# One weight sum of every seven-product group, made in DRAM by a copy and an adding transfer

## The chip, the cores and the metric

One core of one Trainium2 chip runs the whole kernel. The metric is the device time in microseconds of one execution; three executions of the kernel before took 1473.48, 1473.88 and 1474.7 us, the median is 1473.88 us. The profile is of one execution. Its engines are called PE (matrix products), PEld (the load of the stationary operand of a product), DVE, ACT and POOL (elementwise work), and SP (which here issues DMA transfers). SPq, ACTq and POOLq are the instruction queues of those engines.

## The reference

One decoder layer on 256 tokens of width 2048, everything in float32:

```
u = RMSNorm(h);  P = u @ W_in               # 2048 x 12320, split into z | x,B,C | dt | q | k | v
y_ssm = norm(SSD_scan(silu(conv(x,B,C)), softplus(dt)) * silu(z))
y_att = mixture of dilated causal windows over q, k, v     # 16 heads of 128
h = h + RMSNorm(concat(y_ssm, y_att) @ W_out)              # W_out 4096 x 2048
h = h + RMSNorm(relu(RMSNorm(h) @ W_up)^2 @ W_down)        # W_up 2048 x 8192, W_down 8192 x 2048
```

Nearly all of the time goes to the five products with `W_in`, `W_out`, `W_up` and `W_down`, whose weights are all read once.

## The kernel before, in words

**A float32 product in three.** Each weight tile `raw` of 2 x 128 x 512 floats (512 KB, the function `fetch`, one DMA on SP's queue, L149) is split into `hi` (ACT rounds it, L139) and `lo = raw - hi` (DVE, L140). The activations are held split as well. A product is then three matmuls: high by high, high by low, low by high (L262 to L264 in `row_tile`; L393 and L396 in `products`, where the weights are the stationary operand). Four `raw` buffers and five pairs of `hi` and `lo` let DMA, ACT and DVE run ahead of PE by a few tiles.

**Seven products for eight.** A group of the 2 x 2 blocks of 128 tokens and 128 weight rows, by two column blocks of 512, would take eight products. `seven` (L311) takes seven, by the Winograd form of Strassen's scheme: it needs four sums of weights. With `A = raw_a`, `B = raw_b` (the two column blocks `ca` and `cb` of the same two row blocks 0 and 1) DVE makes, in L320 to L325 through `add_in_line` (L225), `e0 = A0 + B0`, `e1 = e0 + B1`, `t4 = e1 + A1`, and in place `B0 = B0 + B1`. Then the tiles A, e, (B0+B1, B1) and t4 are split as above. The combined results are put together by `combine_new` or `combine_onto`. 59 groups are done so: 8 for the values, 9 in `W_out`, 21 in `W_up`, 21 in `W_down`. The others go by `row_tiles`. `unit` runs through one pair of column blocks in a written order of groups.

**The order of the work.** A scheduler sorts the instructions of each engine: higher priority first (`tc.high_priority`), and what depends on data waits by semaphore. `tc.issue_after(i)` adds an order edge behind the instruction `i`, without a semaphore. Each engine then runs its list strictly in order. The first 350 us do the projections for B, C, x, z of the SSD heads, with convolution and scan worked in between; then queries, keys, values and attention; then `W_out`, `W_up` and `W_down`. The first use of `seven` is with the values, some 400 us in.

**Where the step sits that the prediction speaks of.** The first RMSNorm's scale `rstd` is made early: DVE sums (L543) and `rm` (L133), then POOL raises it to the power of -1/2 (L134, in `rsqrt_mean`). `over_partitions` (L546) spreads it: DVE makes `dg` from `rstd` (L551), PE multiplies `ones` by `dg` (L552), DVE copies the result to `rbc` (L553). The convolution (`conv`, L652) uses `rbc` for every block; it has POOL set three columns of `pad` to zero (L655) and DVE do the rest. POOL has 67 instructions in all. It issues no DMA in the kernel before.

Of the kernel before, what the change touches and what calls it, by code (L numbers as in the profile page):

```python
# [10 lines left out]
F32 = mybir.dt.float32  # L11
# [3 lines left out]
ALU = mybir.AluOpType  # L15

P = 128
# [20 lines left out]
COL_V = COL_K + NH * DH  # L38
NB = 512
KB = 2  # L40
MASKED = -1.0e30
PAIRS = ((128, 1), (512, 4), (2048, 16))
AHEAD = 1_000_000
# [7 lines left out]
FIRST = 3  # L51
UP_SEVENS = (2, 4, 5)
V_SEVENS = (1, 3, 5, 6)


def constants():
# [18 lines left out]
def hymba_layer(ctx: ExitStack, tc: tile.TileContext, x, norm_mix_pre, w_in, conv_w, conv_b, dt_bias, a_log,  # L75
                d_skip, ssm_norm_w, w_out, norm_mix_post, norm_mlp_pre, w_up, w_down, norm_mlp_post,
                consts, out):
    nc = tc.nc
    w_in, w_out, w_up, w_down = w_in[0], w_out[0], w_up[0], w_down[0]
# [61 lines left out]
        return (nc.scalar.activation(hi, src, AF.Copy, scale=scale),  # L141
                nc.vector.scalar_tensor_tensor(lo, src, scale, hi.bitcast(F32), op0=ALU.mult, op1=ALU.subtract))

    def fetch(src, k0, c0, step=KB, into=None):

        raw = wp.tile([P, KB, NB], F32, name="raw", bufs=RAWS) if into is None else into
        for j in range(0, KB, step):
            rs = slice((k0 + j) * P, (k0 + j + step) * P)
            nc.sync.dma_start(raw[:, j:j + step], src[rs, c0:c0 + NB].rearrange("(k p) n -> p k n", p=P))  # L149
        return raw  # L150
# [13 lines left out]
    room = {}  # L164
# [22 lines left out]
        room["acts"] = acts  # L187
        sums_of.clear()

    def fetch_next(src, k0, c0):  # L190

        if room["raw"] is None:
            return fetch(src, k0, c0)
        turn = room["turn"]
        room["turn"] += 1
        n = KB * (turn % (RAWS + (NK - SUMS) // KB - 1) - RAWS)
        return fetch(src, k0, c0, into=None if turn < 0 or n < 0 else room["raw"][:, n:n + KB])

    def parts():
        return [wp.tile([P, KB, NB], F32R, name=n, bufs=BUFS) for n in ("hi", "lo")]  # L200
# [2 lines left out]
    product = {}  # L203
# [5 lines left out]
    line = {}  # L209
# [10 lines left out]
        with in_line():  # L220
            line["act"], line["dve"] = split(hi, lo, raw)

    def add_in_line(dst, a, b):
        with in_line():
            line["dve"] = nc.vector.tensor_tensor(dst, a, b, op=ALU.add)  # L225

    def weights(src, k0, c0, fetch=fetch):

# [82 lines left out]
    def seven(src, ca, cb, k, acc, more, first, last):  # L311


        ch, cl = sums_of_acts(k)
        h_, l_, r = room["acts"](k * KB)
        with tc.high_priority(offset=AHEAD):
            raw_a = fetch_next(src, k * KB, ca)
            raw_b = fetch_next(src, k * KB, cb)
            e, t4 = sum_tile(), tmp()
            add_in_line(e[:, 0], raw_a[:, 0], raw_b[:, 0])  # L320
            add_in_line(e[:, 1], e[:, 0], raw_b[:, 1])
            hl_a = parts()
# [12 lines left out]

        def summed(i):
            return ch[:, i], cl[:, i]

        for dst, (a_h, a_l), (hi, lo), j, own in (
                (more[0], block(0, 0), hl_a, 0, True), (acc[0], block(1, 0), hl_a, 1, False),  # L340
                (more[1], summed(1), hl_e, 0, True), (more[2], summed(2), hl_e, 1, True),
                (more[3], summed(0), hl_b, 0, True), (acc[1], summed(3), hl_b, 1, False),
                (acc[2], block(1, 1), hl_t, 0, False)):
            nc.tensor.matmul(dst, a_h, hi[:, j], start=own and first, stop=False)  # L344
            nc.tensor.matmul(dst, a_h, lo[:, j], start=False, stop=False)  # L345
            nc.tensor.matmul(dst, a_l, hi[:, j], start=False, stop=own and last)  # L346
# [12 lines left out]
    def order_of(ks, by_seven):  # L359
        return [(k, k in by_seven) for k in ks]  # L360
# [445 lines left out]
    def keys_too(hb):  # L806
        return queries(COL_Q + hb * NB, rbq), queries(COL_K + hb * NB, rbc)
# [11 lines left out]
    def two_values(vb):  # L819

        if vb:
            room["own"] = deque(mp.tile([P, NT, NB], F32, name="tk", bufs=3)[:, t] for t in range(NT))
        room["sum"] = mp.tile([P, 4, S], F32, name="cT", bufs=5).rearrange("p (k f) s -> p k (f s)", k=KB)
        values = [mp.tile([P, NT, NB], F32, name="tk", bufs=3) for _ in range(2)]
        more = [psmall(), bank(), psmall(), bank()]
        acc = [bank() for _ in range(2 * NT)]

        def end(b):
            def at_end(t, a):
                with tc.high_priority(offset=AHEAD):  # L830
# [5 lines left out]
        unit(w_in[:, COL_V:], vb, order_of(range(7), V_SEVENS), (7,), acc, more,  # L836
             lambda x: combine_new([[v[:, t] for t in range(NT)] for v in values], x), 0, (end(0), end(1)))
        return values

# [236 lines left out]

    in_place_of_u()
    acc = [bank() for _ in range(2 * NT)]
    early = 5
    for k in range(early):  # L1080
# [31 lines left out]
    def whole(n):  # L1112
        def at_end(t, a):
# [1 line left out]
                mixed(n, t, a)  # L1115
        return at_end

    unit(w_out, 0, order_of(range(early, 14), (6, 9, 12)), (14, 15), acc, more,
         lambda x: combine_new(in_mw(0), x), 0, (whole(0), whole(1)), first=False)
    for n in (2, 3):  # L1120
        load_wpost(norm_mix_post, n)
    acc, more = more, acc
# [9 lines left out]
    def first_hidden(t, acc):  # L1132
# [11 lines left out]
    unit(w_out, 2, order_of((0, 6, 1, 9, 2, 12, 3, 4, 5, 8, 7, 10), (6, 9, 12, 4, 8, 10)), (11, 13, 14, 15), acc, more,  # L1144
         lambda x: combine_new(in_mw(2), x), ending=mix_to_up)
    begun = ended.pop()
    over_partitions(rbc, rmlp)
# [88 lines left out]
    for hf in range(2):  # L1236
        if hf:
            in_place_of_h(act_u)
        for fb in range(0 if hf else 2, 8, 2):
            unit(w_up[:, hf * 4096:], fb, order_of(range(6), UP_SEVENS), (6, 7), acc, more,  # L1240
                 lambda x: combine_new(room["shared"], x), 0, (up_end(fb, 0), up_end(fb + 1, 1)))
            acc, more = more, acc
        if hf == 0:
            in_place_of_h(part)
            unit(w_down, 0, order_of(range(14), (4, 6, 9, 11, 13)), (14, 15), acc, more,
                 lambda x: combine_new(in_mw(0), x), 0, (onto(0), onto(1)))
            unit(w_down, 2, order_of((0, 1, 4, 2, 6, 3, 9, 5, 11, 7, 13, 8), (4, 6, 9, 11, 13)), (10, 12, 14, 15), more, acc,
                 lambda x: combine_new(in_mw(2), x), 0, (onto(2), onto(3)))
    new_h()

# [11 lines left out]
    in_place_of_u()  # L1262
    for n in range(2):
        load_wpost(norm_mlp_post, n)
    unit(w_down[4096:], 0, order_of(range(14), (3, 6, 8, 11, 13)), (14, 15), acc, more,
         lambda x: combine_onto(0, x), 0, (complete(0), complete(1)))
    for n in (2, 3):
        load_wpost(norm_mlp_post, n)
    waiting.append(copies(of_h, in_dram, 1))
    unit(w_down[4096:], 2, order_of((0, 1, 3, 2, 6, 4, 8, 5, 11, 7, 13, 9), (3, 6, 8, 11, 13, 9)), (10, 12, 14, 15), more, acc,  # L1270
         lambda x: combine_onto(2, x), LAG_DOWN, (complete(2), finish))


# [21 lines left out]
```

## Time and profile before

| | |
|---|---|
| median of three runs | 1473.88 us |
| span of the profiled execution, first to last instruction | 1471.1 us |
| own time of the profiled execution | not listed apart; the three timed runs stand 2.4 to 3.6 us above the span |
| PE busy | 1461.2 us |
| DVE busy | 1239.6 us |
| ACT busy | 861.1 us |
| POOL busy | 47.8 us |
| bytes moved by DMA | 287.31 MB |

A row of a group reads: line, engine, operation, output and input tiles, shapes, number of instructions, then busy time and the mean of one in ns, then the idle time of the engine just before them and who ended it. A row of a timeline reads: start, length, engine, line, operation, and in brackets the idle time ahead of it and its releaser. A row of the stretches reads: from and to, length, then busy time and number of instructions of PE, PEld, DVE, ACT and POOL, the granted clock, the DMA engines' busy share, and GB/s. Busy time of PE runs up to modelled ends of its pipelined matmuls.

### The profile page before, as it was taken

Reading aid. Unit: us, or ns where it says so; the run is one execution under the profiler, and the core shown is the slowest. Engines: PE = TensorE matmul, PEld = TensorE weight load, DVE = VectorE, ACT = ScalarE, POOL = GpSimd, SP = SyncE. Lnnn points to the kernel's source line nnn. Section 1 sums busy time; section 2 is a strip of 40 time slices with the busy share of each in tenths; the row PEclk is TensorE's granted clock in tenths of the full one; section 3 lists DMA queues with packets and bytes.
Section 4 is the critical chain, followed back from the end, with each engine's and each line's share of the span. In section 5 each row is a group of like instructions: output and inputs, shape, how many; then the busy total and the mean of one; then the engine's idle time right before and its main releaser. Section 6 shows DMA issues by size and latency. Waiting matters only on the chain.

```text
span 1471.1 us, 20006 instructions
## 1 busy us (share of the span) xinstructions
PE 1461.2 (99%) x7216; PEld 1231.4 (84%) x7216; DVE 1239.6 (84%) x1849; ACT 861.1 (59%) x1188; POOL 47.8 (3%) x67
## 2 busy tenths in 40 slices
PE   9999999999999999999999999999999999999998
PEld 8888888888888888888888888888888888888886
DVE  6798797898497696588989989889887898989998
ACT  7475675465456565555557566655554666665553
POOL 0003100210000000000000000000000000000000
PEclk9999999999999999999999999999999999999999
DMA  7665566555657476566657566655665666576853
GB/s 272 208 205 182 179 184 194 174 172 167 177 168 207 122 208 192 191 229 210 204 177 237 165 194 201 210 175 191 213 223 174 201 201 205 172 235 202 273 200 114
DMA packets 151299, 287.31 MB, mean 195 GB/s; under 512 B 11696, under 2 KB 14624, under 8 KB 151200
## 3 DMA queue, kind: packets, MB, share of 16 engines
q1 hardware_dynamic: 143472, 272.50, 58.9%
q10 hardware_dynamic: 7728, 13.54, 2.8%
q8 instruction: 56, 0.92, 0.3%
q14 instruction: 43, 0.35, 0.1%
HBM read 281.78 MB, written 4.23 MB: 194 GB/s over the span
## 4 chain that ended last, share of the span: by engine, by line
PE 94%; DVE 3%; issue 1%; ACT 1%; DMA 1%; POOL 0%; POOLq 0%; SPq 0%; ACTq 0%; DVEq 0%
PE acc L393 17%; PE acc L262 12%; PE acc L263 12%; PE acc L264 12%; PE acc L396 9%; PE acc L345 4%; PE acc L346 4%; PE acc L344 4%; PE ps L263 3%; PE ps L262 3%; PE ps L264 3%; PE ps L346 2%; PE ps L344 2%; PE ps L345 2%; DVE lo L140 1%
## 5 line engine op out<-in xcount | busy, mean ns | idle before, releaser
L139 ACT ACTIVATE hi<-raw 128x1024 fp32r<-128x1024 f32 (+1 forms) x477 | 499.0, 1053 | 387.9 <-PE acc L393 111.9
L140 DVE TENSOR_TENSOR lo<-raw,hi 128x1024 fp32r<-128x1024 f32 (+1 forms) x477 | 579.9, 1220 | 135.7 <-ACT hi L139 127.9
L393 PE MATMUL acc<-ua,hi 128*128 128x512 f32 x680 | 186.3, 402 | 0.0
L393 PEld LDWEIGHTS acc<-ua,hi 128*128 128x128 f32 x680 | 119.7, 189 | 18.7
L262 PE MATMUL acc<-hi,ua 128*128 128x512 f32 x280 | 112.0, 400 | 0.0
L396 PEld LDWEIGHTS acc<-ua,lo 128*128 128x128 f32 x680 | 99.8, 189 | 11.6
L264 PE MATMUL acc<-hi,ua 128*128 128x512 f32 x280 | 109.3, 391 | 0.0
L263 PE MATMUL acc<-lo,ua 128*128 128x512 f32 x280 | 109.3, 390 | 0.0
L396 PE MATMUL acc<-ua,lo 128*128 128x256 f32 x680 | 102.9, 281 | 0.0
L262 PE MATMUL acc<-hi,sh 128*128 128x512 f32 x224 | 88.7, 397 | 0.0
L264 PE MATMUL acc<-hi,sl 128*128 128x512 f32 x224 | 87.3, 390 | 0.0
L263 PE MATMUL acc<-lo,sh 128*128 128x512 f32 x224 | 87.3, 390 | 0.0
L139 ACT ACTIVATE hi<-e 128x1024 fp32r<-128x1024 f32 x51 | 54.1, 1062 | 55.5 <-DVE e L225 50.3
L393 PE MATMUL acc<-uc,hi 128*128 128x512 f32 x272 | 77.6, 398 | 0.0
L263 PE MATMUL acc<-lo,ah 128*128 128x512 f32 x168 | 65.5, 390 | 0.4 <-DVE lo L140 0.4
L264 PE MATMUL acc<-hi,al 128*128 128x512 f32 x168 | 65.4, 389 | 0.0
L262 PE MATMUL acc<-hi,ah 128*128 128x512 f32 x168 | 65.4, 389 | 0.0
L264 PEld LDWEIGHTS acc<-hi,ua 128*128 128x128 f32 x280 | 52.6, 188 | 11.6
L140 DVE TENSOR_TENSOR lo<-e,hi 128x1024 fp32r<-128x1024 f32 x51 | 62.0, 1216 | 0.0
L262 PEld LDWEIGHTS acc<-hi,ua 128*128 128x128 f32 x280 | 52.6, 188 | 10.4 <-ACT ua L141 0.3
L263 PEld LDWEIGHTS acc<-lo,ua 128*128 128x128 f32 x280 | 52.7, 188 | 10.0
L264 PE MATMUL acc<-hi,uc 128*128 128x512 f32 x144 | 56.0, 389 | 0.0
(475 smaller groups left out, 3060.9 us busy)
## 6 DMA issues: line engine op xcount, KB each, us to landing
raw<-in_w_in_dram SPq DMA_DIRECT2D x189, 512.0 KB, 3.6
raw<-in_w_up_dram SPq DMA_DIRECT2D x128, 512.0 KB, 3.9
raw<-in_w_down_dram SPq DMA_DIRECT2D x110, 512.0 KB, 4.7
raw<-in_w_out_dram SPq DMA_DIRECT2D x46, 512.0 KB, 4.2
uc<-in_w_out_dram SPq DMA_DIRECT2D x18, 512.0 KB, 4.5
uc<-in_w_down_dram SPq DMA_DIRECT2D x18, 512.0 KB, 5.1
bc<-acs_d ACTq DMA_DIRECT2D x8, 512.0 KB, 4.5
xs<-in_x_dram SPq DMA_DIRECT2D x8, 256.0 KB, 6.3
```

Source lines behind the costliest of these rows:

```text
L139: return (nc.scalar.activation(hi, src, AF.Copy), nc.vector.tensor_tensor(lo, src, hi.bitcast(F32), op=ALU.subtract))
L140: nc.vector.tensor_tensor(lo, src, hi.bitcast(F32), op=ALU.subtract))
L262: nc.tensor.matmul(dst, a_h[:, r, ts], hi[:, j], start=begin and j == 0, stop=False)
L263: nc.tensor.matmul(dst, a_h[:, r, ts], lo[:, j], start=False, stop=False)
L264: product[t] = nc.tensor.matmul(dst, a_l[:, r, ts], hi[:, j], start=False, stop=end and j == KB - 1)
L344: nc.tensor.matmul(dst, a_h, hi[:, j], start=own and first, stop=False)
L345: nc.tensor.matmul(dst, a_h, lo[:, j], start=False, stop=False)
L346: nc.tensor.matmul(dst, a_l, hi[:, j], start=False, stop=own and last)
L393: nc.tensor.matmul(acc[f], hi[:, j, f * P:(f + 1) * P], u(k0 + j), start=k0 + j == 0, stop=False, skip_group_check=True)
L396: nc.tensor.matmul(acc[f][:, 0], lo[:, j, f * P:(f + 1) * P], u(k0 + j)[:, 0], start=False, stop=k0 + j == NK - 1, skip_group_check=True)
```

## The change

The sum `B0 + B1` of every `seven` is not made by DVE. For each group `next_pair` asks POOL's queue for two transfers: a copy of the 128 x 512 block `B0` from the weights to a tile `d` in DRAM (256 KB), and a second transfer that adds the block `B1` to it. `seven` loads `d` in place of `B0` (a DMA of its own on SP's queue, and one more for `B1`, 256 KB each), and DVE then makes `e1 = A0 + d` and `e0 = e1 - B1`. That is three sums by DVE instead of four, 59 times. `plan` writes down the order in which groups come; four pairs are asked for at first, between the first and the second block of queries and keys, and then one more each time that `seven` fetches one. The copy stands inside `issue_after` edges to the last matmuls of `row_tile`. All calls of `next_pair` but the first four are made inside the `tc.high_priority` block of `seven`, since `pair_of` is an argument there.

```diff
-    def fetch(src, k0, c0, step=KB, into=None):
+    def fetch(src, k0, c0, step=KB, into=None, pair=None):
         raw = wp.tile([P, KB, NB], F32, name="raw", bufs=RAWS) if into is None else into
+        if pair is not None:
+            nc.sync.dma_start(raw[:, 0], pair)
+            nc.sync.dma_start(raw[:, 1], src[(k0 + 1) * P:(k0 + 2) * P, c0:c0 + NB])
+            return raw
...
+    def plan(name, src, n, order, by_seven):
+        orders[name, n] = order_of(order, by_seven)
+        pairs.extend((src, n * NB, k) for k in order if k in by_seven)
+
+    def next_pair():
+        if not pairs:
+            return
+        src, ca, k = pairs.pop(0)
+        cb = slice(ca + NB, ca + 2 * NB)
+        d = dram.tile([P, NB], F32, name=f"pair{len(paired)}")
+        with ExitStack() as order:
+            for t in product:
+                order.enter_context(tc.issue_after(product[t].ins))
+            nc.gpsimd.dma_start(d, src[k * KB * P:(k * KB + 1) * P, cb])
+        nc.gpsimd.dma_start(d, src[(k * KB + 1) * P:(k * KB + 2) * P, cb], accum_op=ALU.add)
+        paired.append((src, ca, k, d))
+
+    def pair_of(src, ca, k):
+        next_pair()
+        s_, c_, k_, d = paired[turn_of["pair"]]
...
+        return d
...
         with tc.high_priority(offset=AHEAD):
             raw_a = fetch_next(src, k * KB, ca)
-            raw_b = fetch_next(src, k * KB, cb)
+            raw_b = fetch_next(src, k * KB, cb, pair_of(src, ca, k))
             e, t4 = sum_tile(), tmp()
-            add_in_line(e[:, 0], raw_a[:, 0], raw_b[:, 0])
-            add_in_line(e[:, 1], e[:, 0], raw_b[:, 1])
+            add_in_line(e[:, 1], raw_a[:, 0], raw_b[:, 0])
+            add_in_line(e[:, 0], e[:, 1], raw_b[:, 1], ALU.subtract)
             hl_a = parts()
             split_in_line(*hl_a, raw_a)
             add_in_line(t4, e[:, 1], raw_a[:, 1])
-            add_in_line(raw_b[:, 0], raw_b[:, 0], raw_b[:, 1])
...
+    for _ in range(PAIRS_AHEAD):
+        next_pair()
     qk.append(keys_too(1))
```

The rest of the diff hands the orders through `plan` to `unit` and changes no group.

More of the change, by code (lines that the diff above doesn't have):

```diff
@@ L40 @@
 KB = 2
+EARLY = 5
 MASKED = -1.0e30
@@ L53 @@
 V_SEVENS = (1, 3, 5, 6)
+PAIRS_AHEAD = 4
 def constants():
@@ L196, in fetch_next @@
         n = KB * (turn % (RAWS + (NK - SUMS) // KB - 1) - RAWS)
-        return fetch(src, k0, c0, into=None if turn < 0 or n < 0 else room["raw"][:, n:n + KB])
+        return fetch(src, k0, c0, into=None if turn < 0 or n < 0 else room["raw"][:, n:n + KB], pair=pair)
     def parts():
@@ L221, in split_in_line, with add_in_line, order_of @@
             line["act"], line["dve"] = split(hi, lo, raw)
-    def add_in_line(dst, a, b):
+    def add_in_line(dst, a, b, op=ALU.add):
         with in_line():
-            line["dve"] = nc.vector.tensor_tensor(dst, a, b, op=ALU.add)
+            line["dve"] = nc.vector.tensor_tensor(dst, a, b, op=op)
+    pairs = []
+    w_v, w_ups, w_downs = w_in[:, COL_V:], [w_up[:, hf * 4096:] for hf in range(2)], [w_down, w_down[4096:]]
+    orders = {}
+    def order_of(ks, by_seven):
+        return [(k, k in by_seven) for k in ks]
+    def plan(name, src, n, order, by_seven):
[13 more added lines that the diff above has]
+        paired.append((src, ca, k, d))
+    paired = []
+    def pair_of(src, ca, k):
+        next_pair()
+        s_, c_, k_, d = paired[turn_of["pair"]]
+        assert (s_ is src) and (c_, k_) == (ca, k), (c_, k_, ca, k)
+        turn_of["pair"] += 1
+        return d
+    turn_of = {"pair": 0}
     def weights(src, k0, c0, fetch=fetch):
@@ L834, in end @@
             return at_end
-        unit(w_in[:, COL_V:], vb, order_of(range(7), V_SEVENS), (7,), acc, more,
+        unit(w_v, vb, orders["v", vb], (7,), acc, more,
              lambda x: combine_new([[v[:, t] for t in range(NT)] for v in values], x), 0, (end(0), end(1)))
@@ L1078, in hymba_layer @@
     acc = [bank() for _ in range(2 * NT)]
-    early = 5
-    for k in range(early):
+    for k in range(EARLY):
         for b in range(2):
@@ L1116, in whole @@
         return at_end
-    unit(w_out, 0, order_of(range(early, 14), (6, 9, 12)), (14, 15), acc, more,
+    unit(w_out, 0, orders["out", 0], (14, 15), acc, more,
          lambda x: combine_new(in_mw(0), x), 0, (whole(0), whole(1)), first=False)
@@ L1142, in first_hidden @@
         split(sh[:, 0:4, ts], sl[:, 0:4, ts], p.rearrange("p (f s) -> p f s", f=4))
-    unit(w_out, 2, order_of((0, 6, 1, 9, 2, 12, 3, 4, 5, 8, 7, 10), (6, 9, 12, 4, 8, 10)), (11, 13, 14, 15), acc, more,
+    unit(w_out, 2, orders["out", 2], (11, 13, 14, 15), acc, more,
          lambda x: combine_new(in_mw(2), x), ending=mix_to_up)
@@ L1239, in hymba_layer @@
         for fb in range(0 if hf else 2, 8, 2):
-            unit(w_up[:, hf * 4096:], fb, order_of(range(6), UP_SEVENS), (6, 7), acc, more,
+            unit(w_ups[hf], fb, orders[("up", hf), fb], (6, 7), acc, more,
                  lambda x: combine_new(room["shared"], x), 0, (up_end(fb, 0), up_end(fb + 1, 1)))
@@ L1264, in hymba_layer @@
         load_wpost(norm_mlp_post, n)
-    unit(w_down[4096:], 0, order_of(range(14), (3, 6, 8, 11, 13)), (14, 15), acc, more,
+    unit(w_downs[1], 0, orders[("down", 1), 0], (14, 15), acc, more,
          lambda x: combine_onto(0, x), 0, (complete(0), complete(1)))
@@ L1269, in hymba_layer @@
     waiting.append(copies(of_h, in_dram, 1))
-    unit(w_down[4096:], 2, order_of((0, 1, 3, 2, 6, 4, 8, 5, 11, 7, 13, 9), (3, 6, 8, 11, 13, 9)), (10, 12, 14, 15), more, acc,
+    unit(w_downs[1], 2, orders[("down", 1), 2], (10, 12, 14, 15), more, acc,
          lambda x: combine_onto(2, x), LAG_DOWN, (complete(2), finish))
```

22 lines of the change are left out of this document (16 added, 6 removed).

## The prediction

> **What bounds the kernel now.** I read the page's head and busy times first, then PE's list of waits, then a piece of PE's timeline inside a seven-product group.
>
> ```profile
> span 1471.1 us, 20006 instructions
> ...
> PE 1461.2 (99%) x7216; PEld 1231.4 (84%) x7216; DVE 1239.6 (84%) x1849; ACT 861.1 (59%) x1188; POOL 47.8 (3%) x67
> ...
> PE 94%; DVE 3%; issue 1%; ACT 1%; DMA 1%; POOL 0%; POOLq 0%; SPq 0%; ACTq 0%; DVEq 0%
> ```
>
> The span is 1471.1 us; the timed runs' median, 1473.88, stands 2.8 us above it. PE is busy for 1461.2 us, and 94% of the chain that ended last is PE. Busy time of PE is modelled, so I look at the starts:
>
> ```profile
> 1010.90 0.39 PE L344 MATMUL acc<-hi,ah 128*128 128x512 f32 x1
> 1011.13 0.39 PE L345 MATMUL acc<-lo,ah 128*128 128x512 f32 x1
> 1011.36 0.39 PE L346 MATMUL acc<-hi,al 128*128 128x512 f32 x1
> ```
>
> A matmul starts every 0.23 us, also inside `seven`, back to back. And PE's waits for other engines are these, longest first:
>
> ```profile
> PE ps L1168 <- ACT dg L1167: 2.3, 1, 2.3
> PE ps L444 <- DVE half L433: 1.1, 1, 1.1
> PE ps L961 <- DVE ha L952: 0.9, 1, 0.9
> PE acc L263 <- DVE lo L140: 0.4, 1, 0.4
> PE acc L345 <- DVE lo L140: 0.3, 1, 0.3
> ```
>
> PE waits 0.7 us in all for a `lo` of DVE, though DVE is 84% busy. So PE's stream of matmuls is the bound, and DVE's share is hidden under it. The change leaves the number of matmuls as it is.
>
> **What it removes.** One addition of this row per group:
>
> ```profile
> L225 DVE TENSOR_TENSOR raw<-raw 128x512 f32<-128x512 f32 x54 | 36.8, 682 | 0.0
> ```
>
> ```profile
> L225 DVE TENSOR_TENSOR uc<-uc x5: 678/682/685, 689.9 to 1427.5; 128x512 f32<-128x512 f32 x5
> ```
>
> 59 groups (54 and, in the tile `uc`, 5) by 0.682 us are 40 us of DVE. Beside a PE that waits 0.7 us for `lo`, they are worth at most that: I take 0, with -0.7 as the end. The remaining three additions keep their length and order. The second DMA of SP costs an issue of 0.37 us (L149's row, below) by 59, 22 us of a queue that mostly waits for buffers: 0. The bytes into SBUF are the same.
>
> **What it adds, and where.** The trace of before has no DMA from POOL and none with an addition. What decides is where these stand. In the built program of after, POOL's list (line numbers of the changed file; 256 is the copy, 257 the adding transfer, 136 is the old L134) begins so after its constants:
>
> ```
> L256 DMACopy pair<-in_w_in    x4
> L257 DMACopy pair<-in_w_in    x4   each waits for its own copy
> L256 DMACopy pair<-in_w_out   x4
> L257 DMACopy pair<-in_w_out   x4   each waits for its own copy and for the adding transfer four before
> ...                                (13 such rounds of 4 + 4)
> L256 DMACopy pair<-in_w_down  x3
> L136 TensorTensor rstd<-rm,half
> ```
>
> The order edges of `issue_after` go to matmuls, and PE's list isn't POOL's: no copy carries a wait for PE. With `seven`'s priority and nothing to wait for, 55 of the 59 pairs have moved to the front of POOL's list: 55 copies and 52 adding transfers, "some groups ahead" by up to 1400 us. Only the first four pairs keep their place. Behind all this stands `rstd`, the scale of the first norm. In before:
>
> ```profile
> 38.45 0.70 POOL L134 TENSOR_TENSOR rstd<-rm,half 128x2 f32<-128x2 f32 x1 [2.45 <-DVE rm L133]
> ...
> 46.94 0.28 DVE L551 TENSOR_SCALAR dg<-cst,rstd 128x128 f32<-128x128 f32 x1
> ```
>
> `rstd` was there at 39 us and DVE used it at 47 us. In the built list of after, DVE's `dg` stands behind the 36th `lo` instead of the 19th, and PE's L552 stands after the 20th matmul of L264, at the place that before's PE reached here:
>
> ```profile
> 97.10 0.39 PE L262 MATMUL acc<-hi,ub 128*128 128x512 f32 x1
> 97.32 0.39 PE L263 MATMUL acc<-lo,ub 128*128 128x512 f32 x1
> 97.55 0.39 PE L264 MATMUL acc<-hi,ub 128*128 128x512 f32 x1
> ```
>
> So PE can do 97 us of before's work without `rstd`. If POOL comes to it at a time T later than that, DVE stands at `dg`, every later `lo` is queued behind it on DVE, and PE stops when its tiles are used up. The delay is T - 97, plus the catching up after it. Slower weights before T don't add to it; they only eat into the same wait.
>
> **T, from both sides.** Nearest rows: SP's issue; the queue that carries the weights, and transfers of 256 KB (the first `xs`, then into DRAM, out of DRAM, to the output) with us to landing last; and the first stretches, with the DMA engines' share and GB/s last:
>
> ```profile
> L149 SPq DMA_DIRECT2D raw<-in_w_in_dram x195: 367/368/690, 1.7 to 569.6; - x195
> ```
>
> ```profile
> q1 hardware_dynamic: 143472, 272.50, 58.9%
> ...
> xs<-in_x_dram SPq DMA_DIRECT2D x8, 256.0 KB, 6.3
> ...
> h_d<-ha ACTq DMA_DIRECT2D x6, 256.0 KB, 4.3
> ha<-h_d ACTq DMA_DIRECT2D x6, 256.0 KB, 6.9
> ...
> out_dram<-ha SPq DMA_DIRECT2D x2, 256.0 KB, 2.3
> ```
>
> ```profile
> 0.00:95.00 95.00, 93.79 (x540) 82.31 (x541) 72.00 (x140) 59.30 (x99) 1.53 (x11) 1.00 0.70 225
> ...
> 10.00:20.00 10.00, 10.00 (x63) 8.88 (x62) 7.13 (x12) 7.40 (x16) 0.00 (x0) 1.00 1.05 385
> ```
>
> - Low end: issues cost what SP's cost, transfers land as the fastest row. A round is 8 x 0.37 + 2.3 = 5.3 us; 13 rounds are 69 us, less than 97.
> - By the DMA engines' time: 0.589 x 16 x 1471.1 / 143472 is 96.6 ns for a packet of 2 KB, so 128 rows on 16 engines are 0.77 us. 55 copies are 42 us. An adding transfer has two rows to read for each that it writes; between 0.77 and 1.55 us each, 52 are 40 to 81 us. The weights up to 97 us want 0.70 x 97 = 68 us (the same stretch). With the 16 engines always full, T is 42 + 40 + 68 = 150 us to 42 + 81 + 68 = 191 us.
> - High end: a round takes a copy's landing of 6.9 us and an adding landing of twice that in turn, 20.7 us; 13 rounds are 269 us.
>
> I take T = 170, the middle of the second count, as it is the one that shares the engines with the weights (from 10 to 20 us before's engines are full already, at 385 GB/s). It is an estimate: 1.6 us for each of 107 transfers, while SP's issue took 0.37.
>
> The Trainium skill (Collectives: The Full Stack, section "The bandwidth ceiling: the fold count and why AG ≠ RS ≠ AR") states that a reducing transfer isn't slow by its addition but by two source reads per chunk on the same ring. By that alone T would be 191 and the sum 21 us more; no trace here shows an adding transfer.
>
> **Catching up.** Work of the convolution and of `dt` that DVE did from 47 to 95.6 us now comes after `dg`:
>
> ```profile
> 47.00:95.60 48.60, 48.60 (x278) 42.14 (x277) 42.68 (x94) 28.11 (x39) 0.42 (x4) 1.00 0.60 180
> 95.60:234.00 138.40, 138.40 (x789) 120.87 (x788) 120.39 (x236) 89.00 (x132) 22.56 (x28) 1.00 0.63 190
> ```
>
> The first of these stretches for L140 alone (DVE's busy time and count), and L417's group:
>
> ```profile
> 47.00:95.60 48.60, 19.42 (x17) 1.00 0.60 180
> ```
>
> ```profile
> L417 DVE TENSOR_TENSOR cT<-acc,cT 128x256 f32<-128x256 f32 x64 | 25.7, 418 | 5.9 <-ACT cT L416 5.3
> ```
>
> Of 42.7 us there, 17 `lo` (19.4 us) and eight additions of L417 (about 3) stay: 20 us move. In the next 138.4 us DVE was busy for 120.4, so it has 18.0 us of room for 20, up to the place where the two lists run alike again. I take 8 us of PE waiting; the ends are 2 (20 - 18) and 20 (no room used).
>
> **Sum.** 1471.1 + (170 - 97) + 8 - 0 = 1552 us of span; with 2.8 around it, 1555 us. The ends of the forecast: T = 105 and 8 give 1490; T = 269 and 8 give 1654.
>
> **Rivals.**
> 1. *The queue is short.* T under 97 us: fewer than 0.91 us per transfer. Then there is no wait at `dg`, only the dense DVE of the new order: 0 to 16 us, 1474 to 1490. For it: the low end, 69 us. Against it: the first 256 KB transfers of before, `xs`, take 6.3 us to land, since the engines are full at the start. The Trainium skill (DMA: Bandwidth & Descriptors, section "Anatomy of one DMA — SWDGE (gpsimd) path") gives 2.0 us plus bytes / 436,000 for a transfer from POOL; by it 256 KB take 2.6 us, a round 5.2 and T is 68 us, this rival. Here nothing shows such a transfer, least of all beside a full weight stream.
> 2. *The adding transfers are dear* (each read and write of DRAM in turn, or POOL's own work for a transfer over 2.5 us). T over 269, time over 1655; at 3 us for each of 107 it is 321 and 1706.
> 3. *The other side: faster.* The 40 us of DVE shorten the seven-product stages because a sum there sits ahead of what PE needs, and rival 1 holds with DVE's list bringing no wait. Its price is bounded by PE's waits above: 0.7 us for `lo`, 5 us with all rows. It gives 1469 to 1473, and decides only when T is under 97 and the catch-up is under 1 us.
>
> That the change does not do what it says is in the forecast: sums are made far ahead instead of some groups ahead.
>
> **Chances.** Forecast (1490 to 1655, likeliest 1555) 0.80; rival 1, 0.07; rival 2, 0.09; rival 3, 0.04. A measurement of this kernel tells about 0.2%, 3 us, from no change. Rival 3 is faster by over 0.2% in 0.03; within 0.2% I put 0.01 of it and 0.02 of rival 1, together 0.03; slower is the rest, 0.94. The range that leaves out 2 in 10 is the forecast's own, 1490 to 1655.
>
> **What would show it.** In the profile of after: POOL's `rstd` at about 170 us (right) or before 97 (rival 1); a DVE wait for POOL at `dg` and an idle PE of some 70 us in the first eighth of the span, with nothing like it elsewhere; DMA's share near 1 until then; L225 by 59 fewer; from 350 us on, the same PE stream as before, shifted. The forecast is wrong if PE never waits at L552, or if `rstd` comes late and PE doesn't.

## The result, and the profile after

The changed kernel takes 1581.65 us (median of five runs, 1581.01 to 1584.37); the kernel before, beside it, 1473.49 us. The ratio is 1.0734 (95% interval 1.0721 to 1.0747): slower by 108 us, where 1555 us (82 us slower) was forecast and 1490 to 1655 was the range.

The head of the profile of after, its busy times, three rows of the 40 slices, its DMA queues and its chain:

```profile
span 1579.2 us, 20260 instructions
...
PE 1483.0 (94%) x7216; PEld 1246.7 (79%) x7216; DVE 1207.0 (76%) x1790; ACT 866.3 (55%) x1188; POOL 125.3 (8%) x185
...
PE   6839289999999999999999999999999999999998
...
PEclk9869699999999999999999999999999999999999
DMA  9999886566656664755766666665657566676763
...
q1 hardware_dynamic: 144416, 272.50, 55.4%
q0 software_dynamic: 13216, 30.94, 8.9%
...
PE 84%; issue 6%; DMA 5%; DVE 2%; POOL 2%; ACT 0%; POOLq 0%; DVEq 0%; ACTq 0%
```

PE has the same 7216 matmuls, but it is busy for 94% of the span instead of 99%. The loss has a place: the first five or six slices of 39.5 us, where the DMA engines are full. The granted clock falls to 0.6 in the two slices in which PE is busy for 0.3 and 0.2. Queue q0 is new: POOL's transfers, 30.94 MB, 8.9% of the span on all 16 engines, which is 0.089 x 1579.2 = 140.5 us.

The stretches of after (columns as before: PE, PEld, DVE, ACT, POOL, granted clock, DMA share, GB/s):

```profile
0.00:95.00 95.00, 58.64 (x279) 49.23 (x279) 27.70 (x45) 30.32 (x56) 35.05 (x56) 0.81 1.02 274
95.00:200.00 105.00, 63.94 (x302) 54.83 (x303) 33.03 (x44) 26.76 (x34) 43.29 (x65) 0.76 0.96 243
200.00:300.00 100.00, 90.37 (x494) 76.66 (x493) 88.88 (x198) 61.37 (x91) 18.80 (x28) 0.97 0.66 192
300.00:400.00 100.00, 98.96 (x561) 86.22 (x560) 85.49 (x162) 57.32 (x89) 14.77 (x20) 1.00 0.63 184
```

In the first 95 us PE runs 279 matmuls, where the kernel before ran 540. The DMA engines are 102% and 96% busy in these two stretches, where before they were 70% and 62% busy. From 300 us on PE is full again.

POOL's timeline in after, its beginning and its end (start, length, engine, line, operation, idle time ahead and its releaser):

```profile
1.24 2.32 POOL L256 DMA_DIRECT2D pair<-in_w_in_dram  x4 [0.79 <-POOLq L1338]
6.06 0.88 POOL L257 DMA_DIRECT2D pair<-in_w_in_dram  x1 [2.50 <-DMA pair<-in_w_in_dram]
8.20 0.83 POOL L257 DMA_DIRECT2D pair<-in_w_in_dram  x1 [1.25 <-DMA pair<-in_w_in_dram]
9.27 1.75 POOL L257 DMA_DIRECT2D pair<-in_w_in_dram  x2 [0.24 <-DMA pair<-in_w_in_dram]
10.73 2.40 POOL L256 DMA_DIRECT2D pair<-in_w_out_dram  x4
20.85 1.74 POOL L257 DMA_DIRECT2D pair<-in_w_out_dram  x2 [7.72 <-DMA pair<-in_w_out_dram]
...
171.28 3.09 POOL L256 DMA_DIRECT2D pair<-in_w_down_dram  x4
181.16 3.37 POOL L257 DMA_DIRECT2D pair<-in_w_down_dram  x4 [6.79 <-DMA pair<-in_w_down_dram]
183.56 2.58 POOL L256 DMA_DIRECT2D pair<-in_w_down_dram  x3
185.26 1.73 POOL L136 TENSOR_TENSOR rstd<-rm,half 128x2 f32<-128x2 f32 x1
```

The 13 rounds of four copies and four adding transfers stand there as the built order had them, 14.2 us each (185.26 / 13), and in nearly every round POOL waits 6 to 10 us for a copy to land. `rstd`, made at 38 us before, is made at 185 to 187 us. On DVE:

```profile
187.03 0.48 DVE L605 TENSOR_SCALAR dg<-cst,rstd 128x128 f32<-128x128 f32 x2 [28.90 <-POOL rstd L136]
```

and PE's waits for other engines, longest first:

```profile
PE ps L606 <- DVE dg L605: 30.3, 1, 30.3
PE ps L634 <- DVE wdt L142: 23.6, 1, 23.6
PE ps L672 <- DVE dA L667: 7.1, 1, 7.1
PE ps L528 <- DMA xs<-in_x_dram: 4.4, 2, 2.8
PE acc L447 <- DVE cT L471: 4.1, 1, 4.1
```

The wait for `dg` is the longest, but it is 30.3 us, and the kernel lost 108. The second is a wait for `wdt`, made from `raw_dt`, the small weights of `dt`; that transfer took 30.0 us to land (8.4 us before). Waiting is not all of the loss either. PE is idle for 1579.2 - 1483.0 = 96.2 us, before for 1471.1 - 1461.2 = 9.9, which is 86.3 us more. The other 21.8 us are in its busy time: 1483.0 us instead of 1461.2 for the same 7216 matmuls. Here is PE's stretch from 80 to 100 us, in which it runs nothing, and its products for `dt` behind the wait for `wdt`, which ended at 101.68 us:

```profile
80.00:100.00 20.00, 0.00 (x0) 0.00 (x0) 0.00 (x0) 0.00 (x0) 6.93 (x10) 0.51 0.99 222
```

```profile
107.07 0.41 PE L635 MATMUL ps<-uc,wdt 128*64 128x256 f32 x1
107.28 0.41 PE L634 MATMUL ps<-uc,wdt 128*64 128x256 f32 x1
...
107.66 0.28 PE L634 MATMUL ps<-uc,wdt 128*64 128x256 f32 x1
107.78 0.28 PE L635 MATMUL ps<-uc,wdt 128*64 128x256 f32 x1
```

The granted clock is 0.51 in that stretch. From 101.7 to 107.5 us the products start 0.21 us apart, from 107.7 us on 0.12 us apart. By the trace's clock records PE was busy for 38.7 us at a granted clock of 0.5 (0.1 us before); at half speed that is some 19 us, an estimate. So the waits cost more than their own length, and neither the forecast nor an experiment has a term for that.

How late PE is at each point shows best when the same matmul, counted in PE's order over the loops that multiply weight tiles, is looked up in both traces (worked out from their starts; the other columns are experiments below):

| place, on the clock of before | after | e12_overwrite | e9_early | e3_tiny |
|---|---|---|---|---|
| 35 us | 29.0 us late | 25.7 | 31.2 | 11.1 |
| 52 us (behind `wdt`) | 55.4 | 44.1 | 31.2 | 13.0 |
| 92 us | 59.4 | 41.3 | 36.3 | 73.1 |
| 98 us (behind `dg`, but for e3_tiny) | 92.9 | 58.9 | 89.1 | 74.0 |
| 204 us | 109.9 | 67.7 | 105.7 | 76.3 |

So in after PE is 59 us late (61 at the most) before it ever comes to the scale, the wait for the scale takes it to 93, and the next 100 us to 110. From there on nothing more is lost.

### The profile page after: what moved, and what is told of

Read it like the earlier page. It is cut to its first block, busy times and chain, and to the rows that moved or that the text cites. A ratio compares the mean times of both kernels' runs of the same rounds, so it can differ in the third digit from the quotient of the medians.

```text
span 1579.2 us, 20260 instructions
## 1 busy us (share of the span) xinstructions
PE 1483.0 (94%) x7216; PEld 1246.7 (79%) x7216; DVE 1207.0 (76%) x1790; ACT 866.3 (55%) x1188; POOL 125.3 (8%) x185
## 3 DMA queue, kind: packets, MB, share of 16 engines
q1 hardware_dynamic: 144416, 272.50, 55.4%
q0 software_dynamic: 13216, 30.94, 8.9%
HBM read 312.71 MB, written 35.16 MB: 220 GB/s over the span
## 4 chain that ended last, share of the span: by engine, by line
PE 84%; issue 6%; DMA 5%; DVE 2%; POOL 2%; ACT 0%; POOLq 0%; DVEq 0%; ACTq 0%
PE acc L447 13%; PE acc L309 11%; PE acc L307 11%; PE acc L308 11%; PE acc L450 6%; PE acc L389 4%; PE acc L388 4%; PE acc L390 4%; PE ps L307 3%; PE ps L308 3%; PE ps L309 3%; DMA pair<-in_w_down_dram 2%; PE ps L389 2%; PE ps L388 2%; PE ps L390 2%
## 5 line engine op out<-in xcount | busy, mean ns | idle before, releaser
L447 PE MATMUL acc<-ua,hi 128*128 128x512 f32 x680 | 190.0, 408 | 8.5 <-DVE cT L471 4.1
L450 PE MATMUL acc<-ua,lo 128*128 128x256 f32 x680 | 106.7, 286 | 0.5 <-DVE lo L142 0.5
```

Of the source, the lines that this page charges most:

```text
L447: nc.tensor.matmul(acc[f], hi[:, j, f * P:(f + 1) * P], u(k0 + j), start=k0 + j == 0, stop=False, skip_group_check=True)
L450: nc.tensor.matmul(acc[f][:, 0], lo[:, j, f * P:(f + 1) * P], u(k0 + j)[:, 0], start=False, stop=k0 + j == NK - 1, skip_group_check=True)
```

## Experiments

Two causes offered themselves. **Theory A**, the forecast's: `rstd` stands behind POOL's queue, DVE stops at `dg`, and what happens before only eats into that wait. **Theory B**: the transfers take the DMA engines from the weights when these are needed most, and that costs time wherever no wait covers it. Each expectation spells them out for its run. The kernel before, run beside each of them, took 1473.4 to 1473.5 us.

### Both removed: e1_paced

Five DRAM tiles instead of 59, and each pair of transfers behind POOL's last work of the scan (the first four pairs get the high priority too):

```diff
-        d = dram.tile([P, NB], F32, name=f"pair{len(paired)}")
-        with ExitStack() as order:
-            for t in product:
-                order.enter_context(tc.issue_after(product[t].ins))
+        d = ring[len(paired) % len(ring)]
+        with tc.issue_after(pooled["last"].ins):
             nc.gpsimd.dma_start(d, src[k * KB * P:(k * KB + 1) * P, cb])
-        nc.gpsimd.dma_start(d, src[(k * KB + 1) * P:(k * KB + 2) * P, cb], accum_op=ALU.add)
+            nc.gpsimd.dma_start(d, src[(k * KB + 1) * P:(k * KB + 2) * P, cb], accum_op=ALU.add)
...
```

> The pairs are held behind POOL's last instruction of the scan by an order edge on POOL's own list, and live in five DRAM tiles that are used in turn, so that a copy waits until SP has loaded the tile's last pair: some groups ahead indeed. Theory A (the delay of the changed kernel is rstd standing behind 107 transfers on POOL, to 187 us, and DVE's catching up of 18 us): both are gone, 1472 to 1476 us. Theory B (the delay is the share of the DMA engines that the pairs take, 140 us of all 16 engines in all): they still take it, but spread over 1000 us in which the engines are busy for 0.62, so 1473 to 1480. Both gain at most the 1.2 us that the changed kernel caught up after 450 us.

1473.9 us, ratio 1.0 (0.9991 to 1.0009), in the intervals of both theories. The same 118 transfers, made as the text of the change describes, a few groups ahead, cost nothing and bring nothing. In the stretch where the values are made (340 to 540 us), and after:

```profile
340.00:540.00 200.00, 199.53 (x1057) 171.44 (x1056) 148.01 (x230) 112.36 (x167) 15.57 (x22) 1.00 0.73 206
540.00:1471.00 931.00, 922.97 (x4248) 764.51 (x4246) 777.00 (x1033) 543.13 (x708) 67.80 (x98) 1.00 0.74 226
```

DMA's share is 0.73 and 0.74 (0.60 and 0.62 before), so the pairs find room and PE stays full.

### No wait at rstd, but a burst: e2_late

As e1_paced, but without the ring: 59 tiles, so all pairs start in one burst at 337 us, behind the scan. Against e1_paced the edit is:

```diff
-        d = ring[len(paired) % len(ring)]
+        d = dram.tile([P, NB], F32, name=f"pair{len(paired)}")
```

> All 59 pairs in one burst again, but behind POOL's last instruction of the scan (330 us) instead of ahead of rstd; the four first pairs go first. Nothing of POOL's own work stands behind the burst for the next 400 us. Theory A: 1473 to 1480. Theory B: the burst takes half of the engines beside weights that want 0.6 of them, for some 180 us, and PE falls behind by 30 to 70 us: 1505 to 1545.

1506.44 us, ratio 1.0221 (1.0207 to 1.0235): theory B's interval. `rstd` is made at 38.5 us, POOL has no other work behind the burst until 801 us, and yet 33 us are lost:

```profile
340.00:540.00 200.00, 179.86 (x936) 151.86 (x935) 124.92 (x204) 95.04 (x149) 75.48 (x111) 0.95 1.04 289
```

The DMA engines are full for these 200 us, and PE is busy for 180 of them.

### The order alone: e3_tiny

The same transfers at the same places with 2 KB instead of 256 KB each (the sum is not used):

```diff
-        cb = slice(ca + NB, ca + 2 * NB)
-        d = dram.tile([P, NB], F32, name=f"pair{len(paired)}")
+        cb = slice(ca + NB, ca + NB + 4)
+        d = dram.tile([P, 4], F32, name=f"pair{len(paired)}")
```

> The changed kernel with the same number of copies and adding transfers in the same place ahead of rstd, but of 4 floats a row (2 KB each instead of 256 KB); B0 itself is loaded in place of the sum, so the sum B0 + B1 is left out. The built order puts dg behind the 26th lo (65 us in the kernel before). Theory A: rstd comes after 107 issues of 0.55 to 0.83 us and 13 rounds with two landings of 2 to 3 us each, at 110 to 140 us, so 45 to 75 us of waiting and 5 to 15 of catching up: 1525 to 1560. Theory B: the engines are free, 1473 to 1485.

1547.54 us, ratio 1.049 (1.047 to 1.0509): theory A's interval. With 0.25 MB moved instead of 30.94, `rstd` still comes late:

```profile
129.64 2.58 POOL L257 DMA_DIRECT2D pair<-in_w_down_dram  x3 [4.56 <-DMA pair<-in_w_down_dram]
133.89 1.65 POOL L257 DMA_DIRECT2D pair<-in_w_down_dram  x2 [1.67 <-DMA pair<-in_w_down_dram]
135.04 1.35 POOL L136 TENSOR_TENSOR rstd<-rm,half 128x2 f32<-128x2 f32 x1
```

and the one long wait of PE is that for the scale:

```profile
PE ps L606 <- DVE dg L605: 57.9, 1, 57.9
```

The loss is 74 us, and 63 of them come at the scale: by the same count as in the table PE is 11.7 us late just before it and 74.7 behind it. The other 11 us were lost in the first 25 us, since these transfers are not free of engine time, though theory B took them to be: their 10384 packets take 2.7% of the span on all engines, 42 us, and the engines are 0.89 busy up to 95 us. So this is the order with little engine time, not without any. It also bounds T from below: 13 rounds of issue and landing take 135 us, and the last four, from 90.4 us on, still take 11 us each, though the weights stand still for most of that time (2 GB/s from 95 to 140 us). (In this build `dg` stands further ahead on DVE and PE, at about 65 us of the clock of before instead of 97.)

### The bytes without POOL: e4_bytes and e11_bytes_twice

The kernel before, with copies of 512 KB from `W_down` to DRAM tiles on ACT's queue, two with each of the first weight tiles; no instruction reads what they write. 42 copies in the one, 84 in the other:

```diff
+    def move():
+        for _ in range(2):
+            if len(moved) < 42:
+                n = len(moved)
+                moved.append(dram.tile([P, KB, NB], F32, name=f"moved{n}"))
+                rows, cs = slice(n // 4 * 256, n // 4 * 256 + 256), columns_of(n % 4)
+                nc.scalar.dma_start(moved[n], w_down[rows, cs].rearrange("(k p) n -> p k n", p=P))
...
         with tc.high_priority(offset=AHEAD):
+            move()
             raw = fetch(src, k0, c0)
...
```

> The kernel before (four sums on DVE, no pairs) with 42 copies of 512 KB from DRAM to DRAM beside the first 21 weight tiles, issued from ACT's queue, two a tile; nothing waits for them. At the changed kernel's 203 ns for a 2 KB packet they take 136 us of all 16 engines, about what its pairs took, and POOL's list is that of before. Theory A: rstd is there in time, and only ACT's issues cost: 1474 to 1490. Theory B: PE falls behind by 50 to 80 us while they run: 1525 to 1555.

1522.4 us, ratio 1.0325 (1.0311 to 1.0339): 49 us, just under theory B's interval and far over A's. The copies took 61 us of all 16 engines, not the expected 136 (ACT's queue q10 goes from 2.8% of 1471.1 us to 6.7% of 1520.9).

> The kernel before and 84 copies of 512 KB between DRAM tiles from ACT's queue, two with each of the first 42 weight tiles, twice as many as in e4_bytes (42 copies, 61 us of all 16 engines, cost 49 us); 122 us of engines, somewhat less than the 140 of the changed kernel's transfers; nothing waits for them and no order on POOL or DVE is changed. Theory A (the changed kernel's loss is rstd's wait; transfers beyond the full first stretch find the engines 62% busy and hide): 1520-1545. Theory B (0.8 us lost for each us of engines, however many): 1560-1580.

1561.77 us, ratio 1.0603 (1.0582 to 1.0623): theory B. The stretches of this run:

```profile
0.00:95.00 95.00, 71.51 (x339) 60.87 (x340) 32.72 (x50) 32.53 (x57) 0.21 (x4) 0.89 0.95 336
95.00:200.00 105.00, 82.44 (x357) 64.89 (x357) 34.52 (x34) 29.22 (x35) 0.00 (x0) 0.90 1.03 371
```

122 us of engines cost 88 us (0.72 for one), with POOL's queue as it was; the first 42 copies cost 49 us, the second 42 cost 39. But this is not the bytes alone. In these builds the copies and SP's weight transfers use the same eight semaphores in turn, so that a transfer waits for the one that had its semaphore before. ACT's `hi` stands behind such waits for copies for 80.0 us up to 200 us (32.9 in e4_bytes), and SP's queue for 95.7 us (42.7). `rstd` is made late as well, at 203 us (115 in e4_bytes), though PE has no wait for `dg` in either. What stands is that the engines are full (0.95 and 1.03) while PE falls behind. How much of the loss goes to the added waits is not shown.

### No sum at all: e5_relief

The kernel before without one of its four additions, and nothing in its place, so the weights of one block lack a term:

```diff
-            add_in_line(raw_b[:, 0], raw_b[:, 0], raw_b[:, 1])
```

> The kernel before without the one addition of L225 (59 adds of 0.682 us, 40 us of DVE); nothing is put in its place, so one term of each sum is left out. Theory A (PE bounds the kernel, the relief is hidden): 1472-1474 us, within 0.2% of before. Rival C (DVE's time is worth something where its operations stand in a chain to PE): 1440-1469. It is the most that any way of making this sum for nothing could give.

1471.3 us, ratio 0.9985 (0.9976 to 0.9994): just under theory A's interval and over rival C's. Sums that cost nothing at all would bring 2.1 us. That is the most that the change could win here.

### Copies without additions: e6_copies

The adding transfer is left out; the 55 copies stay ahead of `rstd`, and none waits for a sum. (Against the expectation, each still waits for the copy eight before it; see the last section.)

```diff
-        nc.gpsimd.dma_start(d, src[(k * KB + 1) * P:(k * KB + 2) * P, cb], accum_op=ALU.add)
```

> The changed kernel without the adding transfer: 59 copies alone (the sum lacks its second term). 55 copies stand ahead of rstd on POOL, none waits for another, so POOL is through with issuing them after 55 x 0.54-0.83 = 30-46 us; the scale's matmul stands at its old place, which the kernel before reaches at 55.5 us. Theory A (the wait of rstd behind POOL's list is the whole loss): 1474-1490. Theory B (the DMA engines' time adds where no wait covers it): 59 copies at about 1.6 us of all engines are 95 us, which reach the first weights; as 61 us of the copies on the other queue cost 49 us, these cost 50-80: 1525-1555.

1520.73 us, ratio 1.0317 (1.0301 to 1.0332): below B's interval, far over A's.

```profile
q0 software_dynamic: 4720, 15.47, 3.4%
```

A copy is 0.034 x 1520.4 / 59 = 0.88 us of all engines, not the 1.6 that the expectation had put on it. `rstd` was made at 87.2 us, later than the expected 30 to 46; but POOL had stood idle for 19.2 us ahead of it, waiting for `rm`, so the queue was not what held it, and PE has no wait for `dg`. PE was 48 us late by 35 us of the clock of before and 51 later on. 51.7 us of engines at the start cost 47 us.

### Fewer pairs ahead: e7_half and e10_early_half

24 pairs ahead of `rstd`, four more behind it, the rest paced as in e1_paced:

```diff
+FREE = 28
...
-        d = dram.tile([P, NB], F32, name=f"pair{len(paired)}")
+        d = ring[len(paired) % len(ring)] if len(paired) >= FREE else dram.tile([P, NB], F32, name=f"free{len(paired)}")
...
-            for t in product:
-                order.enter_context(tc.issue_after(product[t].ins))
+            if len(paired) >= FREE:
+                order.enter_context(tc.issue_after(pooled["last"].ins))
             nc.gpsimd.dma_start(d, src[k * KB * P:(k * KB + 1) * P, cb])
-        nc.gpsimd.dma_start(d, src[(k * KB + 1) * P:(k * KB + 2) * P, cb], accum_op=ALU.add)
+            nc.gpsimd.dma_start(d, src[(k * KB + 1) * P:(k * KB + 2) * P, cb], accum_op=ALU.add)
...
```

> The changed kernel with 24 pairs instead of 55 (and 52) ahead of rstd on POOL, six rounds of 4 copies and 4 adding transfers; four more pairs behind it, the other 31 paced behind POOL's last scan operation. The scale's matmul stands at its old place, reached at 55.5 us in the kernel before; six rounds in the changed kernel's trace end at 88.5 us, so rstd's scale is ready at about 91 us. Theory A (the wait is the loss, slower weights before it are covered by it): 91 - 55.5 = 35 us and 0-18 of catching up, 1507-1528. Theory B (the transfers' 24 x 2.4 = 57 us of all DMA engines add to the wait): 1545-1575.

1527.71 us, ratio 1.0367 (1.0352 to 1.0381). The time lies in A's interval, but not for A's reason. DVE in this run:

```profile
97.61 0.69 DVE L145 TENSOR_TENSOR wdt<-raw_dt,wdt 128x512 fp32r<-128x512 f32 x1 [20.41 <-ACT wdt L144]
98.55 3.49 DVE L145 TENSOR_TENSOR lo<-raw,hi 128x1024 fp32r<-128x1024 f32 x3 [0.25 <-ACT hi L144]
101.97 0.47 DVE L609 TENSOR_SCALAR dg<-cst,rstd 128x128 f32<-128x128 f32 x2
```

`rstd` was there at 88.8 us. `dg` comes at 102 us without a wait, because DVE's list had stood at `raw_dt` before it. That called for a second run, with `raw_dt` loaded at the very start:

```diff
+    raw_dt = mp.tile([P, NK, 32], F32, name="raw_dt")
...
+        nc.scalar.dma_start(raw_dt, w_in[:, COL_DT:COL_DT + 32].rearrange("(k p) n -> p k n", p=P))
...
-        raw = sp1.tile([P, NK, 32], F32, name="raw_dt")
-        nc.scalar.dma_start(raw, w_in[:, COL_DT:COL_DT + 32].rearrange("(k p) n -> p k n", p=P))
+        raw = raw_dt
```

> e7_half (24 pairs ahead of rstd) with the same transfer moved to the start. In e7_half's trace rstd is made at 88.8 us but its scale stands on DVE behind the 20.4 us wait for raw_dt, until 102 us, and PE reaches it 51 us late. Theory A (rstd behind POOL's list is e7_half's loss): 1522-1530, unchanged. Theory B (e7_half's loss is that of the slow transfers, raw_dt's 20.5 us and 29 us before it, and rstd would be in time or nearly): 1503-1515.

1513.57 us, ratio 1.0272 (1.0257 to 1.0288): theory B's interval, 14 us less. Where `rstd` comes soon enough, what the transfers cost shows: 24 pairs, some 57 us of engines at the 2.4 us that a pair takes in after, cost 40.

```profile
88.79 1.23 DVE L145 TENSOR_TENSOR lo<-raw,hi 128x1024 fp32r<-128x1024 f32 x1 [2.49 <-ACT hi L144]
89.94 0.48 DVE L613 TENSOR_SCALAR dg<-cst,rstd 128x128 f32<-128x128 f32 x2
```

`dg` stands on DVE without a wait here either, and PE waits 1.8 us for it. Of the 40 us that are left 32 are lost in the first 35 us, where weights and tiles of `x` came late (up to 75 us ACT waits 34.7 us for `raw`, PE 9.1 for `xs`).

### The same edit in the full change: e9_early

`raw_dt` at the start, as in the diff above, in the changed kernel.

> The changed kernel with one transfer moved: the small weights of dt (raw_dt) are loaded at the very start, into a tile of their own, in place of at 70 us, where they took 30.0 us to land and PE waited 23.6 us for what is made of them; the place of the scale's matmul is unchanged. Theory A (the forecast's rule: what is lost before rstd's scale only eats into the same wait): rstd is still made at about 187 us, 1572-1587. Theory B (losses before and at the scale add up): 23 us less, 1553-1565.

1578.4 us, ratio 1.0717 (1.07 to 1.0735), in A's interval. The 23.6 us wait for `wdt` is gone, and the next one has grown:

```profile
PE ps L610 <- DVE dg L609: 49.0, 1, 49.0
```

49.0 instead of 30.3 us. What was won ahead of the scale was waited for at the scale, and only what `rstd` came sooner (its `dg` stands at 183 instead of 187 us) was kept: 3 us.

### Five reused tiles: e8_ring

```diff
-        d = dram.tile([P, NB], F32, name=f"pair{len(paired)}")
+        d = ring[len(paired) % len(ring)]
...
+    ring = [dram.tile([P, NB], F32, name=f"pair{i}") for i in range(PAIRS_AHEAD + 1)]
```

> The changed kernel with the sums in five reused DRAM tiles and nothing else: the reuse holds a copy until a weight tile has taken the sum out, so five pairs stand ahead of rstd on POOL, nothing between the scan's operations, and the rest behind them in its order. Theory A (the wait of rstd is the loss): rstd is made by about 38-40 us as before, 1472-1480. Theory B (DMA engines' time): five pairs are 12 us of all engines at the start, and the paced ones cost nothing beside a stretch whose engines are 60% busy: 1472-1485. Rival D (the reuse puts a new wait between a weight tile and POOL's next copy): over 1490.

1485.35 us, ratio 1.0082 (1.0068 to 1.0095): at the edge of B's interval, over A's, under D's. `rstd` waited for DVE's `rm`, not for a transfer. Five pairs, 12 us of engines, made PE 9.1 us late by 17 us of the clock of before, and some 6 us came in two places later, whose cause was not followed up (the profiled execution took 1488.3 us, 3 above the median).

### The addition alone: e12_overwrite

The second transfer as a plain copy over the first; all waits and places are kept, only the addition goes:

```diff
-        nc.gpsimd.dma_start(d, src[(k * KB + 1) * P:(k * KB + 2) * P, cb], accum_op=ALU.add)
+        nc.gpsimd.dma_start(d, src[(k * KB + 1) * P:(k * KB + 2) * P, cb])
```

> The changed kernel with the second transfer of each pair a plain copy over the first, without the addition (the sum lacks its first term); every wait, order and issue is kept. In the changed kernel's packets the adding transfers are those of 2 KB, 203 ns in the mean (1.6 us of all engines each), the copies those of 4 KB, 185 ns (0.74 us). Theory A (T is set by the engines' time, and the addition's second read doubles it): 52 x 0.85 = 44 us less for the engines, rstd at 143-160 us, 1537-1556. Theory B (T is set by the rounds of issue and landing; the addition costs nothing of its own): rstd at 175-187 us, 1568-1582.

1538.9 us, ratio 1.0446 (1.0429 to 1.0464): theory A's interval, 43 us less than after. POOL at the end of its queue, and the queue's share:

```profile
150.10 0.53 POOL L257 DMA_DIRECT2D pair<-in_w_down_dram  x1 [0.80 <-DMA pair<-in_w_down_dram]
150.61 1.55 POOL L256 DMA_DIRECT2D pair<-in_w_down_dram  x3
152.26 0.74 POOL L136 TENSOR_TENSOR rstd<-rm,half 128x2 f32<-128x2 f32 x1
```

```profile
q0 software_dynamic: 9440, 30.94, 6.2%
```

The same bytes took 0.062 x 1537.0 = 95.3 us of all engines instead of 140.5, and `rstd` came 33 us sooner. The packets bear out which transfer is which: 9440 instead of 13216, and all that are left of 2 KB and more are of 4 KB, so the packets of 2 KB were those of the additions.

## Why the prediction was right, step by step

- **PE is the bound, and the relief of DVE is hidden: right.** Forecast 0, at most 0.7 us; e5_relief measured 2.1 us for sums that are free (interval of the ratio 0.9976 to 0.9994). The term was a little small. In after PE gains 1 to 2 us from 204 us to the end.
- **55 pairs have moved ahead of `rstd`: right**, word for word in POOL's timeline. So was the place where PE comes to the scale: by then it was 59 us late, and it resumed at 187.4 us, which is 187.4 - 97.1 = 90.3 us late.
- **T: 170 forecast, 187 measured, between the two ends of the count it came from (150 and 191).** Both ends can be checked now. The low end gave an adding transfer one read; e12_overwrite is that kernel, and its `rstd` came at 152.3 us. The high end gave it twice that time. A plain transfer is 95.3 / 118 = 0.81 us of all engines (0.77 forecast); 59 of them leave 140.5 - 47.7 = 92.8 us for the adding ones, 1.57 us each (1.55 was the high end). The forecast took the middle where the high end was the truth: this is the term that was mis-sized, 17 of the 27 us. The rule weighed there (the Trainium skill, Collectives: The Full Stack, "The bandwidth ceiling: the fold count and why AG ≠ RS ≠ AR"), that a reducing transfer pays for two source reads, gave 191. The doubled time in this trace and in e12_overwrite agrees with that. The second read itself is not seen: the profile counts 312.71 MB read in both.
- **The low end by issues and landings (69 us): wrong, and without effect.** e3_tiny needs 135 us for rounds with 0.25 MB. Issue took mostly 0.5 to 0.8 us instead of 0.37, and transfers of 256 KB landed after 8 to 10 us in the median instead of 2.3. So T is bounded twice: 135 by the rounds, 152 or 187 by the engines. The 2.6 us for such a transfer, an estimate by the formula of the Trainium skill (DMA: Bandwidth & Descriptors, "Anatomy of one DMA — SWDGE (gpsimd) path"), was not seen beside a weight stream: the shortest landing of a copy in after is 4.5 us. Rival 1 did not come about.
- **"Slower weights before T don't add to it; they only eat into the same wait": right for this kernel.** e9_early shows it directly: 23.6 us taken away ahead of the scale, 18.7 us more of waiting at it. But the forecast's picture of a single wait of some 70 us at L552 was wrong. PE waited 30.3 us there. Of the 59 us of lateness before it 29 were lost in the first 35 us, to weights and tiles of `x` that landed late (up to 75 us ACT waits 33.6 us for `raw`, PE 7.2 for `xs`) and to the lower clock behind such waits, and 26 behind `raw_dt`. The rule holds only while the wait is the longer of the two: in e7_half and e10_early_half it isn't, and there the transfers set the time.
- **Catching up: 8 forecast (2 to 20), 17 to 19 measured** (91 to 93 us late behind the scale, 110 at 204 us on the clock of before). The forecast counted DVE's moved work alone. With the same DVE list but 45 us less engine time, e12_overwrite loses 9 us there (58.9 to 67.7), so about half of it goes with the engine time. By the traces, after, e9_early and e12_overwrite each lose 11.6 us from 150 us of the clock of before on, where DVE is busy for 80.3 of 88 us (232 to 320 us of after) and the DMA engines are 0.57 busy: that is DVE's moved work. Ahead of that after loses 5 us where e12_overwrite wins back 3: ACT waits 5.4 us for a weight tile, DVE 4.3 us for `pad`, which POOL sets behind three more adding transfers, and then PE 7.1 us for `dA`. This term held the other 10 of the 27 us.
- **The sum.** 1471.1 + 90 + 19 - 1 = 1579 us of span, as measured.

What the forecast did not see is that its wait was not the only way to this loss. The order with little engine time costs 74 us (e3_tiny), and 122 us of engines at the start, with POOL's queue as it was, 88 us (e11_bytes_twice, with its own added waits). Together in after they cost 108, not 162, because what is lost ahead of the scale shortens the wait there (e9_early). So the time alone did not confirm the mechanism: e6_copies and e11_bytes_twice, in which PE never waits for the scale, also lie in the range from 1490 to 1655 us. The wait at `dg`, e3_tiny and e9_early confirm it. Had `rstd` been kept out of POOL's queue, much of the loss would probably have stayed; that was not tried, since POOL's other work of the convolution stands behind the same queue.

## What to carry to other kernels

A DMA that depends on nothing goes where priority puts it: before a transfer is put "some groups ahead", read the built list of the queue that issues it, and hold it there by a buffer that must come free or by an edge to an instruction of the same engine. Then price it in time of all DMA engines (share times span), an adding transfer at twice a copy, and ask what share the engines have where it will run: 140 us of engines cost nothing in a stretch at 0.6, 33 us as a burst in that stretch, and 0.7 to 0.9 of their length at the start (0.72 in e11_bytes_twice, 0.91 in e6_copies). And before moving work off an engine, leave it out once: here the whole prize was 2.1 us.

## What the runs showed of the hardware beyond that

- An adding transfer from DRAM to DRAM takes twice the engine time of a copy (1.57 and 0.81 us of all 16 engines for 256 KB). It goes in packets of 2 KB, the copy in packets of 4 KB (the queue's packets: 13216 with additions, 9440 without).
- POOL mostly spends 0.5 to 0.8 us on issuing one such transfer, SP 0.37 us on a weight tile.
- One limit here is the program's and not the chip's: POOL's transfers use eight semaphores in turn, so each waits until the one eight before it has landed. A round of four copies and four adding transfers uses up the eight, and in e6_copies the waits made 55 issues of 0.52 us take 68 us.
- While both queues were at work, POOL's took more of the engines' time for about the same bytes. From 10 to 35 us of after (packets, MB, share):

```profile
q0 software_dynamic: 1576, 3.52, 61.1%
q1 hardware_dynamic: 2534, 3.65, 46.1%
```

- `raw_dt`, a transfer in pieces of 128 bytes on a third queue, landed after 30.0 us instead of 8.4, and after 11.3 us when it was issued at the very start. Why it took so long in after is not shown.
